# A decoder block on one core: the sixth head pair's transposes by VectorE and DMA instead of TensorE, and the out-projection's products ordered by feature halves

## The chip, the cores and the metric

The kernel runs on one core of a Trainium2 chip. Its engines work in parallel, each through its own instructions in order, and wait for each other by semaphores: TensorE (PE in the profile), VectorE (DVE), ScalarE (ACT), GpSimd (POOL) and SyncE (SP). SP and POOL also issue the transfers (DMAs) between the core's memory and HBM. The metric is the device time of one execution in microseconds (us), the median of several runs.

## The reference

One layer of a hybrid decoder: three groups of heads read one input projection, their outputs are concatenated and projected by `w_out`, and a feed-forward part follows. There are 512 tokens, width 1024, hidden width 4096, all in f32.

```python
h = rmsnorm(x, norm1_w)
proj = h @ w_in
aq, ak, av, bq, bk, bv, br, ba, cq, ck, cv = jnp.split(proj, ...)
y_a = dilated_attention(heads(aq, A_HEADS), heads(ak, A_HEADS), heads(av, A_HEADS), bias_a)   # 6 heads of 64
y_b = gla(heads(bq, B_HEADS), heads(bk, B_HEADS), heads(bv, B_HEADS), br, ba, w_a2, b_a, gla_norm_w)   # 4 heads
y_c = moba_attention(heads(cq, C_HEADS), heads(ck, C_HEADS), heads(cv, C_HEADS), bias_c)       # 6 heads of 64
mix = jnp.concatenate([y_a.reshape(Bsz, S, A_WIDTH), y_b, y_c.reshape(Bsz, S, C_WIDTH)], axis=-1)
x = x + mix @ w_out
h2 = rmsnorm(x, norm2_w)
x = x + jnp.square(jax.nn.relu(h2 @ w_ff1)) @ w_ff2
...
return rmsnorm(x, final_norm_w)
```

For 512 tokens both attentions come down to causal softmax attention with a bias table per head: the three dilated branches become one softmax whose bias holds the logarithm of how many branches see a distance, and the block-sparse attention sees every past block.

## The kernel before

**Order of the work.** The program is written as some thirty generators ("streams") that yield instructions, waits and fired events. At build time a planner (`Plan.run`) takes, with estimated costs, the instruction that can start first and issues it. So the order on each engine is fixed when the program is built, and on the chip each engine works through its list. All instructions are issued at one line (L141), which is why the profile's groups are told apart by the names of the tiles.

**Matrix products.** A product in f32 accuracy is made of three faster ones: each operand is cut into a high and a low part (ACT makes the high part: `wh`, `Ah`, `xh`; DVE the low part by a subtraction: `wl`, `Al`, `xl`), and hi x hi, lo x hi and hi x lo are summed in one PSUM bank. The out-projection and the second feed-forward matrix use a scheme with seven block products instead of eight (`products(c)`, c = 0 for the out-projection). Each product has a left operand that is a sum of blocks (`a_parts`, tiles `s`), a right operand that is a sum of weight blocks (`sums0`, tiles `t` and `b`; cut in `cut2`), and a bank X, W or Y in which it accumulates (`f2X`, `f2W`, `f2Y` in the profile). `add` puts a bank's result on the residual tiles `x3`, which the profile calls `x`. Each product runs over two halves of its inner dimension, `ip` = 0 and 1, 12 matmuls each.

**Attention.** The twelve heads of the two softmax attentions run as six pairs p, with e = 0, 1 in a pair. For each head `attention` makes the scores on PE (`sps`) and `softmax` the exponentials in tiles `P` (queries on partitions). For the product with the values, P has to be transposed. For the pairs in `XP` (0 to 4) this is `moved`: DVE transposes blocks of 32x32 (`tb`, `t2s`), SP writes them to HBM (`turn`), and POOL reads them back so that the blocks end up in transposed order (`thb`, `th`; twelve DMAs a pair, in `back`). Pair 5 takes the other way: PE transposes into a bank (`ptp`, 10 blocks for each of the two heads), and ACT copies it out (`turned`). The row sums go through HBM too (`zt`, `rzb`).

**Values.** `values` takes two pairs at a time: it waits for their transposes, takes banks "o" and "g" (`po` in the profile), runs the products, and `mix_out` (DVE) scales them by `rzb` into the mix tiles `h`. The features of the mix are in the order `KO`: feature block 6 is pair 4, block 7 is pair 5, and both are needed only in `ip` = 1 of the lower half.

**After it.** When a residual tile is final, `x2_out` makes the norm (`ssq`, `y`), PE transposes the normalized rows (`y_out`, `yps`), and the feed-forward part begins (`ff1_first`, bank `f`).

SP's list also holds all loads of weights (`woraw` for the out-projection, `wraw`, `w1raw`, `w2raw` for the feed-forward part) and of the residual, in `fetch`, `fetch0`, `fetch1` and `fetch2`. A DMA of SP also waits until the eighth one before it has landed, where that has not yet been waited for (SP has eight semaphores in turn).

Of the kernel before, what the change touches and what calls it, by code (L numbers as in the profile page):

```python
# [29 lines left out]
NC = 5  # L30
ZL, PL = 4.5, 3.2
XP = (0, 1, 2, 3, 4)
# [177 lines left out]
def hybrid_block_kernel(ctx: ExitStack, tc: tile.TileContext, x0_d, xT_d, x_d, w0_d, wv_d, wqk_d, w1_d, w2_d,  # L210
# [81 lines left out]
    def fetch():  # L292
        for key, src, n in pieces[1:]:
# [211 lines left out]

    def cut2(c):
        for o, (n, *_) in enumerate(products(c)):
# [6 lines left out]
            for ip in range(2):  # L514
                yield from parts(("2", c, n, ip), B[c][n][ip])
            fire(("cut2", c, n))
# [434 lines left out]
    def values():  # L951


        for ps_ in ((0, 1), (2, 3), (4, 5)):
# [35 lines left out]
            for _ in range(4 + (ps_[0] == 0) + 2 * (ps_[0] == 4)):  # L990
# [30 lines left out]
    def moved(p, e, P):  # L1021
# [19 lines left out]
        yield from back(th, d)  # L1041
        if both:
            yield from back(th2, d2)
# [179 lines left out]
    def x2_out(t, half):  # L1223
        both = t in ssq
        yield from square_sum(t, half)
        if both:
# [6 lines left out]
            scaled.append(t)  # L1233
            if len(scaled) == NT:
# [14 lines left out]
    def y_out(t, half, y0):  # L1249
        r = (("pt", "pt"), ("o", "g"))[t % 2][half]  # L1250
# [83 lines left out]
    def a_parts(c):  # L1334
# [4 lines left out]
        def split(n, src, sign=1):  # L1339
            for ip in range(2):  # L1340
# [38 lines left out]
        if not c:  # L1379
            yield ("wait", ("v", 1, 0))  # L1380
            yield ("prio", 1)
        yield from ready(0, 0)
# [3 lines left out]
        if not c:  # L1386
            yield ("wait", ("values", 2))
            yield ("prio", 0.5)
# [7 lines left out]
        if c:  # L1396
            yield from split(1, q10)
        yield from ready(1, 1)
        yield from urgent(3)
        if c in (0, NC - 1):  # L1400
            yield from split(6, q11)
        yield from urgent(4)
        s1 = yield from made("s1", q01, q11, OP.subtract if c else OP.add)
# [4 lines left out]
        yield from split(3, s1, -1 if c else 1)  # L1408
        give("big")
        yield from urgent(6)  # L1410
        if not c:
            yield from split(1, q10)
            s4 = yield from made("s4", q10, s2, OP.subtract)
        else:
            yield ("take", "big")
            s4 = big("s4", F32, (128, 2, 2, 256))
            s4 = [s4[:, ip] for ip in range(2)]
            for ip in range(2):
                yield DVE.scalar_tensor_tensor(s4[ip], q10[ip], -1.0, s2[ip], op0=OP.mult, op1=OP.subtract)
# [464 lines left out]
```

## Time and profile before

| | |
|---|---|
| median of 3 runs | 557.39 us (556.43 to 557.56) |
| the profiled execution | 556.4 us |
| its span, first to last instruction | 554.6 us |
| TensorE clock granted | 0.997 |
| PE busy | 546.1 us, 98% |
| DVE busy | 488.0 us, 88% |
| ACT busy | 351.2 us, 63% |
| POOL busy | 84.6 us, 15% |
| moved by DMA | 101.44 MB, mean 183 GB/s |

The profiled execution is 1.0 us below the median of the runs and 1.8 us longer than its span, so times from the trace are compared with 556.4, and a difference is then taken over to the median. A row of the trace gives an instruction's start and duration; matmuls overlap in the pipeline, so what one costs is read from start to start, or from a piece of the chain divided by its count (the profile counts a matmul of f32 operands twice, with x80 for 40).

### The profile page before, as it was taken

How to read it: one execution, taken by the hardware profiler on the slowest of the kernel's cores; microseconds unless marked ns; L12 is line 12 of the kernel's file. 1: busy time of each engine (PE TensorE's matmuls, PEld its weight loads, DVE VectorE, ACT ScalarE, POOL GpSimd, SP SyncE). 2: the span in 40 equal slices, each digit the busy share in tenths (PEclk: the TensorE clock that was granted, in tenths of full speed). 3: DMA queues.
4: the chain of work that ended last, by engine and by line, in shares of the span. 5: the costliest groups of instructions: out<-in, count | busy, mean ns of one | idle time of the engine just before them, and what ended most of it. 6: DMA issues, size and time to landing. Idle time of an engine off the chain costs nothing.

```text
span 554.6 us, 9438 instructions
## 1 busy us (share of the span) xinstructions
PE 546.1 (98%) x3530; PEld 484.8 (87%) x3530; DVE 488.0 (88%) x793; ACT 351.2 (63%) x588; POOL 84.6 (15%) x135
## 2 busy tenths in 40 slices
PE   9999999999999999999999999999999999999995
PEld 8987888888888888999988999988999888999884
DVE  6969998999987899899899858999589999588986
ACT  7746465668576546768855448864377753479654
POOL 7100000431524001100111100111000111202031
PEclk9999999999999999999999999999999999999998
DMA  8930304699998969803679714688815788937504
GB/s 314 392 136 2 110 6 132 215 281 253 273 285 275 316 201 376 171 1 115 152 157 281 212 72 153 152 221 234 228 38 190 160 223 230 212 79 209 106 1 152
DMA packets 33518, 101.44 MB, mean 183 GB/s; under 512 B 5026, under 2 KB 5712, under 8 KB 33472
## 3 DMA queue, kind: packets, MB, share of 16 engines
q1 hardware_dynamic: 24816, 73.76, 39.3%
q0 software_dynamic: 8368, 26.53, 24.5%
q8 instruction: 28, 0.46, 0.3%
q10 hardware_dynamic: 288, 0.53, 0.3%
q14 instruction: 18, 0.15, 0.1%
HBM read 92.11 MB, written 8.71 MB: 182 GB/s over the span
## 4 chain that ended last, share of the span: by engine, by line
PE 98%; DVE 1%; issue 0%; ACT 0%; DVEq 0%
PE f2X L141 19%; PE f1V L141 15%; PE qkps L141 12%; PE f2W L141 10%; PE vps L141 8%; PE f1W L141 7%; PE f2Y L141 5%; PE f L141 4%; PE f1X L141 4%; PE sps L141 3%; PE po L141 2%; PE av L141 2%; PE lp L141 1%; PE bk L141 1%; PE bq L141 1%; PE op L141 1%
## 5 line engine op out<-in xcount | busy, mean ns | idle before, releaser
L141 POOL DMA_DIRECT2D w2raw<-in_w x36 | 31.7, 907 | 301.9 <-DVE wl L141 199.1
L141 DVE TENSOR_TENSOR wl<-w2raw,wh 128x1024 fp32r<-128x1024 f32 x56 | 68.4, 1238 | 2.6 <-ACT wh L141 2.6
L141 ACT ACTIVATE wh<-w2raw 128x1024 fp32r<-128x1024 f32 x56 | 58.2, 1050 | 17.3 <-PE f2Y L141 12.5
L141 PE MATMUL f2X<-wh,Ah 128*128 128x512 f32 (+1 forms) x160 | 62.3, 390 | 0.0
L141 PE MATMUL f2X<-wh,Al 128*128 128x512 f32 (+1 forms) x160 | 61.9, 387 | 0.0
L141 PE MATMUL f2X<-wl,Ah 128*128 128x512 f32 (+1 forms) x160 | 61.9, 387 | 0.0
L141 ACT ACTIVATE wh<-w1raw 128x1024 fp32r<-128x1024 f32 x42 | 43.3, 1051 | 29.2 <-DVE w1raw L141 27.6
L141 DVE TENSOR_TENSOR wl<-w1raw,wh 128x1024 fp32r<-128x1024 f32 x42 | 50.8, 1222 | 12.3 <-ACT wh L141 12.3
L141 PE MATMUL f1V<-Uh,wl 128*128 128x256 f32 x168 | 47.6, 283 | 0.0
L141 PE MATMUL f1V<-Ul,wh 128*128 128x256 f32 x168 | 47.6, 283 | 0.0
L141 PE MATMUL f1V<-Uh,wh 128*128 128x256 f32 x168 | 47.6, 283 | 0.0
L141 ACT ACTIVATE h<-h 128x512 f32<-128x512 f32 x53 | 33.3, 629 | 17.8 <-DVE h L141 17.1
L141 PE MATMUL qkps<-xh,wh 128*128 128x512 f32 x96 | 38.1, 397 | 0.0
L141 PE MATMUL qkps<-xh,wl 128*128 128x512 f32 x96 | 37.5, 390 | 0.0
L141 PE MATMUL qkps<-xl,wh 128*128 128x512 f32 x96 | 37.5, 390 | 0.0
L141 ACT ACTIVATE P<-P,mn 128x512 f32<-128x512 f32 (+3 forms) x48 | 26.6, 556 | 15.6 <-DVE mn L141 15.4
L141 PEld LDWEIGHTS f2X<-wh,Ah 128*128 128x128 f32 x160 | 30.1, 188 | 6.9 <-issue 1.0
L141 DVE TENSOR_TENSOR wl<-wraw,wh 128x1024 fp32r<-128x1024 f32 (+1 forms) x32 | 34.5, 1087 | 1.5 <-ACT wh L141 1.4
L141 PEld LDWEIGHTS f2X<-wl,Ah 128*128 128x128 f32 x160 | 30.1, 188 | 6.1
L141 PEld LDWEIGHTS f2X<-wh,Al 128*128 128x128 f32 x160 | 30.1, 188 | 5.8
L141 ACT ACTIVATE Ah<-s 128x512 fp32r<-128x512 f32 x40 | 23.8, 623 | 15.8 <-DVE s L141 15.3
L141 PEld LDWEIGHTS f1V<-Uh,wh 128*128 128x128 f32 x168 | 32.3, 192 | 0.0
(297 smaller groups left out, 1675.7 us busy)
## 6 DMA issues: line engine op xcount, KB each, us to landing
w2raw<-in_w SPq DMA_DIRECT2D x42, 512.0 KB
w2raw<-in_w POOLq DMA_DIRECT2D x36, 512.0 KB, 7.0
w1raw<-in_w SPq DMA_DIRECT2D x28, 512.0 KB
wraw<-in_wqk SPq DMA_DIRECT2D x12, 512.0 KB
turn<-tb SPq DMA_DIRECT2D x10, 512.0 KB
thb<-turn POOLq DMA_DIRECT2D x40, 128.0 KB, 5.9
wraw<-in_wv SPq DMA_DIRECT2D x8, 512.0 KB
woraw<-in_w SPq DMA_DIRECT2D x8, 512.0 KB
```

The lines of the kernel that those rows point to most:

```text
L141: getattr(getattr(self.nc, op.eng), op.method)(*op.args, **op.kw)
```

## The change

- `XP` now holds pair 5 too: its blocks are transposed by DVE, written to HBM by SP, and read back, and there are no `ptp` transposes on PE and no copies from them on ACT. For this pair alone the twelve read-backs are issued by SP, not by POOL (`back`).
- `values` runs pairs 0 and 1, then 2 and 3 together, then pair 4 alone and pair 5 alone, the last two both in bank "o".
- The out-projection's products are cut into halves of the inner dimension where that matters (`segments`): 0 and 4 whole, then 6, 2 and 1 with `ip` = 0, then 6 and 2 with `ip` = 1, 3 whole, 1 with `ip` = 1, 5 whole. `cut2`, `ff2` and `a_parts` (a new `mixed_parts` for c = 0) follow that order, and the sums `s` are made half by half.
- Product 1's bank Y is now of kind "pt" (free, since `ptp` is gone) and no longer "s"; `y_out` swaps its two pairs of banks.
- The loads of the second half of the residual wait for pair 4's read-backs instead of for its values; the cut of one feed-forward weight tile waits until the fourth token tile is scaled; `half_dense` waits for its weight half only where it uses it.

```diff
-XP = (0, 1, 2, 3, 4)
+XP = (0, 1, 2, 3, 4, 5)
...
             if key[0] == "x3":
-                yield ("wait", ("values", 4 if key[2] else 2))
+                yield ("wait", ("thx", 4) if key[2] else ("values", 2))
...
             yield ("wait", ("raw", key))
+            if key == ("1", 0, 0, 1):
+                yield ("wait", ("scaled", 3))
...
+    def segments(c):
+
+        at = {n: o for o, (n, *_) in enumerate(products(c))}
+        return [(at[n], n, ips) for n, ips in (((0, (0, 1)), (4, (0, 1)), (6, (0,)), (2, (0,)), (1, (0,)), (6, (1,)), (2, (1,)), (3, (0, 1)), (1, (1,)), (5, (0, 1))) if not c else [(n, (0, 1)) for n in at])]
+
     def cut2(c):
-        for o, (n, *_) in enumerate(products(c)):
+        for o, n, ips in segments(c):
...
-        for ps_ in ((0, 1), (2, 3), (4, 5)):
+        for ps_ in ((0, 1), (2, 3), (4,), (5,)):
...
-    def back(dst, d):
+    def back(dst, d, p):
         n = d.shape[1]
         for k in range(4):
-            yield POOL.dma_start(dst[k * 32:k * 32 + 32].rearrange("p (a c) -> p a c", a=4),
+            yield (SP if p > 4 else POOL).dma_start(dst[k * 32:k * 32 + 32].rearrange("p (a c) -> p a c", a=4),
...
-        r = (("pt", "pt"), ("o", "g"))[t % 2][half]
+        r = (("o", "g"), ("pt", "pt"))[t % 2][half]
...
+            for _, n, ips in segments(0)[2:]:
+                for ip in ips:
+                    for i in range(2):
+                        yield ("wait", ("h", 0, 4 + 2 * ip + i))
+                    q10, q11 = (hs[0][1, ip][:, half] for half in range(2))
+                    if n == 2:
+                        yield DVE.tensor_tensor(s[1][ip], q01[ip], q11, op=OP.add)
+                        yield DVE.tensor_tensor(s[2][ip], s[1][ip], q00[ip], op=OP.subtract)
+                    if n == 5:
+                        yield DVE.tensor_tensor(s[4][ip], q10, s[2][ip], op=OP.subtract)
+                    yield from split(n, {6: (q11, q11), 1: (q10, q10)}.get(n) or s[{2: 2, 3: 1, 5: 4}[n]], ips=(ip,))
...
-        return (dict(X="mm", Y="s", W="s") if not c else dict(X="s", Y="mm", W="pt") if c < NC - 1 else dict(X="s", Y="pt", W="mm"))[b]
+        return (dict(X="mm", Y="pt", W="s") if not c else dict(X="s", Y="mm", W="pt") if c < NC - 1 else dict(X="s", Y="pt", W="mm"))[b]
...
         def half_dense(f, j):
             for k in range(KT):
                 kh = k // 4
+                yield ("wait", ("w", ("1", 0, f // 2, kh)))
...
-                for kh in range(2):
-                    yield ("wait", ("w", ("1", 0, f // 2, kh)))
...
-            for o, (n, b_, new, _) in enumerate(products(c)):
+            seens = {}
+            for o, n, ips in segments(c):
+                _, b_, new, _ = products(c)[o]
```

What that does to the orders is shown at three places. On PE, before, the values of pairs 4 and 5 stood together inside product 0 of the out-projection (the rows after `th_2009` are pair 5's, in wide products):

```order
L141 MATMUL f2X<-wl,Ah 128x512
L141 MATMUL po<-thb,v 64x128 x16
L141 MATMUL po<-th_2009,v 64x128 x4
L141 MATMUL po<-th,v 64x256 x2
L141 MATMUL po<-thb,v 64x384 x2
L141 MATMUL po<-thb,v 64x128 x2
L141 MATMUL po<-thb,v 64x512 x2
L141 MATMUL f2X<-wh,Ah 128x512
```

Now pair 4's values stand inside product 4, behind its ninth matmul, and pair 5's at its end, ahead of the first half of product 6. These are the rows around pair 5's (`th_2125` is pair 5's):

```order
L141 MATMUL f2W<-wh,Al 128x512
L141 MATMUL f2W<-wl,Ah 128x512
L141 MATMUL po<-thb,v 64x128 x16
L141 MATMUL po<-th_2125,v 64x128 x4
L141 MATMUL f2W<-wh,Ah 128x512
```

The values of the last two pairs moved from product 0 to product 4, fifteen matmuls of 512 columns apart from each other.

On SP, before, in the stretch behind the writes of pair 4 (`turn_2086` is its last; `x` are the residual's loads):

```order
L141 DMA turn_2086<-t2s 128x512
L141 DMA zt_2122<-rzt_99 8x32 x4
L141 DMA zt_2201<-rzt_101 8x32 x4
L141 DMA woraw<-in_w 128x1024 x2
L141 DMA rzb<-zt_2122 64x512 x2
L141 DMA rzb<-zt_2201 64x512 x2
L141 DMA x_2320<-in_x 128x512
```

And now (`turn_2164`, `turn_2195` and `turn_2204` are pair 5's):

```order
L141 DMA zt_2121<-rzt_99 8x32 x4
L141 DMA turn_2164<-tb 128x1024
L141 DMA woraw<-in_w 128x1024 x2
L141 DMA turn_2195<-tb 128x1024
L141 DMA turn_2204<-t2s 128x512
L141 DMA zt_2213<-rzt_101 8x32 x4
L141 DMA thb<-turn_2164 32x4x256 x4
L141 DMA rzb<-zt_2121 64x512 x2
L141 DMA thb<-turn_2195 32x4x256 x4
L141 DMA th_2125<-turn_2204 32x4x128 x4
L141 DMA x_2305<-in_x 128x512
```

The first load of the residual now stands behind three writes and twelve read-backs of pair 5; its row waits, by the eight semaphores, for the first read-back of `turn_2195`.

On DVE, before, from the copies of the values of pairs 2 and 3 to those of pairs 4 and 5 (`h<-po`):

```order
L141 TENSOR_TENSOR h<-po,rzb 128x2x256 x2
L141 TENSOR_TENSOR s_2319<-h 128x512 x2
L141 TENSOR_TENSOR wl<-b_2321,wh 128x1024
L141 TENSOR_TENSOR Al<-s_2319,Ah 128x512 x2
L141 TENSOR_TENSOR h<-po,rzb 128x2x256 x2
L141 TENSOR_TENSOR x_2320<-f2X,x_2320 128x512
```

And now, from the sums `s` behind the copies of pairs 2 and 3 to the copy of pair 4:

```order
L141 TENSOR_TENSOR s_2304<-h 128x512 x2
L141 TENSOR_TENSOR b_2314<-woraw,t_2170 128x1024
L141 TENSOR_TENSOR Al<-s_2304,Ah 128x512 x2
L141 TENSOR_TENSOR wl<-b_2308,wh 128x1024
L141 TENSOR_TENSOR Al<-h,Ah 128x512
L141 TENSOR_TENSOR s_2367<-h 128x512
L141 TENSOR_TENSOR wl<-t_2145,wh 128x1024
L141 TENSOR_TENSOR x_2305<-f2X,x_2305 128x512
L141 TENSOR_TENSOR x_2320<-f2X,x_2320 128x512
L141 TENSOR_TENSOR s_2368<-s_2367,h 128x512
L141 TENSOR_TENSOR Al<-s_2368,Ah 128x512
L141 TENSOR_TENSOR h<-po,rzb 128x2x256
```

The copy of pair 4 out of bank "o" now stands behind two adds of the residual, and PE's values of pair 5 wait for that copy.

More of the change, by code (lines that the diff above doesn't have):

```diff
@@ L513, in cut2 @@
             yield ("wait", ("B", c, n))
-            for ip in range(2):
+            for ip in ips:
                 yield from parts(("2", c, n, ip), B[c][n][ip])
+            if 1 not in ips:
+                continue
             fire(("cut2", c, n))
@@ L989, in values @@
             yield ops
-            for _ in range(4 + (ps_[0] == 0) + 2 * (ps_[0] == 4)):
+            for _ in range(2 * len(ps_) + (ps_[0] == 0) + 2 * (ps_[0] == 5)):
                 give("big")
@@ L1233, in x2_out @@
             scaled.append(t)
+            fire(("scaled", t))
             if len(scaled) == NT:
@@ L1337, in new, with split @@
             return slot(name, dt, (128, 2, 256))
-        def split(n, src, sign=1):
-            for ip in range(2):
+        def split(n, src, sign=1, ips=(0, 1)):
+            for ip in ips:
                 yield ("take", "part")
@@ L1377, in give_h, with mixed_parts @@
             give("big")
-        if not c:
+        def mixed_parts():
             yield ("wait", ("v", 1, 0))
             yield ("prio", 1)
+            yield from ready(0, 0)
+            yield from ready(0, 1)
+            q00, q01 = quad(0, 0), quad(0, 1)
+            yield from split(0, q00)
+            yield ("wait", ("values", 2))
+            yield ("prio", 0.5)
+            s3 = yield from made("s3", q00, q01, OP.subtract)
+            yield from split(4, s3)
+            give("big")
+            s = {}
+            for n in (1, 2, 4):
+                yield ("take", "big")
+                s[n] = big(f"s{n}", F32, (128, 2, 2, 256))
+                s[n] = [s[n][:, ip] for ip in range(2)]
+            for _, n, ips in segments(0)[2:]:
+                for ip in ips:
+                    for i in range(2):
[7 more added lines that the diff above has]
+                    yield from split(n, {6: (q11, q11), 1: (q10, q10)}.get(n) or s[{2: 2, 3: 1, 5: 4}[n]], ips=(ip,))
+                if n == 2 and 1 in ips:
+                    give_h()
+                if n == 3 and 1 in ips:
+                    give("big")
+            give("big")
+            give("big")
+            give_h()
+        if not c:
+            yield from mixed_parts()
+            return
         yield from ready(0, 0)
@@ L1395, in a_parts @@
         q10, q11 = quad(1, 0), quad(1, 1)
-        if c:
-            yield from split(1, q10)
+        yield from split(1, q10)
         yield from ready(1, 1)
         yield from urgent(3)
-        if c in (0, NC - 1):
+        if c == NC - 1:
             yield from split(6, q11)
         yield from urgent(4)
-        s1 = yield from made("s1", q01, q11, OP.subtract if c else OP.add)
+        s1 = yield from made("s1", q01, q11, OP.subtract)
         s2 = yield from made("s2", s1, q00, OP.subtract)
@@ L1407, in a_parts @@
         yield from urgent(5)
-        yield from split(3, s1, -1 if c else 1)
+        yield from split(3, s1, -1)
         give("big")
         yield from urgent(6)
[L1411 to L1419, printed above, removed]
+        yield ("take", "big")
+        s4 = big("s4", F32, (128, 2, 2, 256))
+        s4 = [s4[:, ip] for ip in range(2)]
+        for ip in range(2):
+            yield DVE.scalar_tensor_tensor(s4[ip], q10[ip], -1.0, s2[ip], op0=OP.mult, op1=OP.subtract)
         give("big")
@@ L1422, in a_parts @@
         give("big")
-        if c not in (0, NC - 1):
+        if c != NC - 1:
             yield from split(6, q11)
@@ L1709, in ff2 @@
                     elif m == 3:
-                        spawn(add(c, o, q, [bk[b_, q][h_] for h_ in js], [cut_[q][h_] for h_ in js]), -1 if end else 1 if c else 0)
+                        spawn(add(c, o, q, [bk[b_, q][h_] for h_ in js], [cut_[q][h_] for h_ in js]), -1 if end else 1 if c else 2 if n == 1 else 0)
     def main():
```

13 lines of the change are left out of this document (5 added, 8 removed).

## The prediction

> **What bounds the kernel now.** I read the page's busy shares and its chain first, then the waits of PE (TensorE), then busy time by stretches around the change, then the chain and the timelines of DVE (VectorE), SP and POOL in those stretches. The first fence has lines of the page (the one of ACT is used further down) and the one wait of PE outside the start.
>
> ```profile
> span 554.6 us, 9438 instructions
> PE 546.1 (98%) x3530; PEld 484.8 (87%) x3530; DVE 488.0 (88%) x793; ACT 351.2 (63%) x588; POOL 84.6 (15%) x135
> ...
> PE 98%; DVE 1%; issue 0%; ACT 0%; DVEq 0%
> ...
> L141 ACT ACTIVATE Ah<-s 128x512 fp32r<-128x512 f32 x40 | 23.8, 623 | 15.8 <-DVE s L141 15.3
> ...
> PE vps L141 <- ACT rg L141: 0.6, 1, 0.6
> ```
>
> PE is the bound, and nothing holds it up: 98% of the chain that ended last is its matmuls. So work taken off PE is worth its full time, as long as no new wait opens. Whether one opens is read from the stage that the change touches (busy time by stretches):
>
> ```profile
> core 0: us, PE busy (x) PEld busy (x) DVE busy (x) ACT busy (x) POOL busy (x), PEclk, DMA share, GB/s
> 160.00:175.00 15.00, 15.00 (x82) 12.83 (x81) 12.97 (x37) 11.63 (x34) 3.14 (x6) 1.00 0.88 284
> 175.00:185.00 10.00, 10.00 (x105) 8.62 (x105) 8.88 (x9) 4.40 (x5) 3.37 (x7) 1.00 1.01 245
> 185.00:195.00 10.00, 10.00 (x81) 7.43 (x80) 8.22 (x12) 7.09 (x9) 0.00 (x0) 1.00 1.04 370
> 195.00:210.00 15.00, 15.00 (x68) 12.43 (x67) 15.00 (x23) 6.90 (x13) 0.00 (x0) 1.00 0.62 201
> 210.00:225.00 15.00, 15.00 (x72) 12.50 (x71) 15.00 (x27) 9.97 (x23) 2.73 (x3) 1.00 1.01 355
> ```
>
> DVE has no gap at all from 195 to 225 us, and the DMA engines are full (share about 1.0) from 175 to 195. The change adds work to both and takes work from PE. The pieces of the chain there:
>
> ```profile
> 170.90 0.66 PE ptp L141 x6
> ...
> 179.52 0.68 PE f2X L141 x3
> 180.20 4.52 PE po L141 x80
> 184.72 1.58 PE f2X L141 x6
> 186.30 4.49 PE po L141 x56
> 190.78 3.67 PE f2X L141 x15
> 194.45 10.88 PE f2W L141 x48
> ...
> 221.65 0.87 PE yps L141 x8
> ```
>
> **PE's part.** Removed: the 20 transposes `ptp` of pair 5. Six take 0.66 us, 0.11 each, so 20 take 2.2 us. Changed: pair 5's values are now 20 narrow products instead of 8 wide ones. Pairs 2 and 3 need 4.52 us for both in the narrow form, 2.26 a pair; pairs 4 and 5 took 4.49 with one pair wide. So this costs nothing. Added: pairs 4 and 5 now interrupt the f2 products one at a time, three interruptions instead of two. A product of 512 columns takes 10.88/48 = 0.227 us; the six behind the first interruption took 1.58 instead of 1.36, the fifteen behind the second 3.67 instead of 3.40. So one more interruption costs 0.2 us. The products ordered by feature halves are the same 168 matmuls. PE's work: -2.2 + 0.2 = **-2.0 us**.
>
> **DVE's part.** Added: eight block transposes, four for each of the two heads. Their starts, and those of what follows, for pair 4 and in the last row of pair 5:
>
> ```profile
> 158.39 0.71 DVE L141 STREAM_TRANSPOSE tb<-P 128x512 f32<-128x512 f32 x1
> 159.02 0.65 DVE L141 TENSOR_TENSOR Al<-h,Ah 128x512 fp32r<-128x512 f32 x1
> ...
> 162.81 0.57 DVE L141 STREAM_TRANSPOSE tb<-P 128x384 f32<-128x384 f32 x1
> 163.31 0.40 DVE L141 STREAM_TRANSPOSE t2s<-P 128x256 f32<-128x256 f32 x1
> 163.63 0.27 DVE L141 STREAM_TRANSPOSE tb<-P 128x128 f32<-128x128 f32 x1
> 163.83 0.52 DVE L141 CUSTOM_DVE_ANT_0 P<-sps,nb 128x384 f32<-128x384 f32 x1
> ```
>
> Start to start they take 0.63, 0.50, 0.32 and 0.20, together 1.65 a head and 3.3 for the pair. Nothing is taken from DVE: the evictions of `ptp` were ACT's. What can cover 3.3 us is DVE's idle time ahead of its full stretch:
>
> ```profile
> 168.50 1.23 DVE L141 TENSOR_TENSOR t<-woraw 128x1024 f32<-128x1024 f32 x1 [0.29 <-DMA woraw<-in_w]
> ...
> 175.79 1.22 DVE L141 TENSOR_TENSOR wl<-woraw,wh 128x1024 fp32r<-128x1024 f32 x1 [2.22 <-ACT wh L141]
> ...
> 179.20 2.35 DVE L141 TENSOR_TENSOR t<-t,woraw 128x1024 f32<-128x1024 f32 x2
> 181.47 2.35 DVE L141 TENSOR_TENSOR b<-woraw,t 128x1024 f32<-128x1024 f32 x2
> ...
> 184.76 0.69 DVE L141 TENSOR_TENSOR h<-po,rzb 128x512 f32<-128x512 f32 x1 [0.34 <-PE po L141]
> 185.37 1.28 DVE L141 TENSOR_TENSOR s<-h 128x512 f32<-128x512 f32 x2
> ...
> 190.83 0.69 DVE L141 TENSOR_TENSOR h<-po,rzb 128x512 f32<-128x512 f32 x1 [1.24 <-PE po L141]
> 191.73 0.69 DVE L141 TENSOR_TENSOR x<-f2X,x 128x512 f32<-128x512 f32 x1 [0.21 <-PE f2X L141]
> ...
> 194.49 0.69 DVE L141 TENSOR_TENSOR x<-f2X,x 128x512 f32<-128x512 f32 x1 [0.33 <-PE f2X L141]
> ```
>
> The brackets add up to 4.63 us. So the transposes fit, but DVE gets ahead of its old schedule by at most 4.63 - 3.3 = 1.3 us, while PE wants to get ahead by 2.0. At the end of the full stretch PE takes the rows `y` of the norm at 221.65 us, and there is little slack there. Between those bounds, 1.3 and 2.0, I take 1.6 us, nearer to DVE's: DVE's row is the one without a gap. ACT loses evictions and is not short of time.
>
> **SP and the wait that it can bring.** Now SP issues three writes of pair 5 and twelve read-backs. All of them stand ahead of the eight loads of `x` (the residual), which stood at 177.47. Timelines of SP and POOL, and the landing times of pair 4's twelve read-backs (least, median, most):
>
> ```profile
> 145.65 0.33 SPq L141 DMA_DIRECT2D turn<-tb  x1
> ...
> 177.47 4.45 SPq L141 DMA_DIRECT2D x<-in_x  x4
> ```
> ```profile
> 152.22 0.55 POOL L141 DMA_DIRECT2D thb<-turn  x1 [2.70 <-DMA turn<-tb]
> ```
> ```profile
> DMA to landing us min/median/max: 2.9/7.6/8.4
> ```
>
> A write of 512 KB was issued at 145.65 and its read-back at 152.22, 6.6 us later. When do pair 5's last transposes end? In DVE's new order five of the eight stand ahead of the sum `t` that started at 168.50, and the last three behind it: 168.50 - 0.29 of idle + 2.28 + 1.13 (`t`) + 1.02 = 172.6. So read-backs could issue from 179.2; I take 181, since two 512 KB loads of the out-projection's weights now stand between the two heads' writes. SP's first `x` waits until the first read-back of the second head has landed (its row waits on that DMA's semaphore): 181 + 7.6 = 188.6. It lands 2.9 us later at the earliest, 191.5, or 8.4 later, 197. With every step at its short end it would be 179.2 + 2.9 + 2.9 = 185.0. I take 192, near the short end of the last step, because the traffic is then thinning out.
>
> Who waits for that: PE starts its f2X at 179.52 - 2.2 = 177.3. By the prices above: 0.68 + 4.52 + 21 x 0.227 = 187.3, nine f2W to 189.3, pair 4's values with the 0.2 to 191.8, fifteen f2W to 195.2. There pair 5's values need bank "o", which DVE must first empty of pair 4's, and in DVE's new order two adds of `x` stand ahead of that. DVE gets to the rows `s` at 185.37 - 2.85 of idle (0.29 + 2.22 + 0.34) - 1.13 (one sum `b` that moves behind) + 3.3 = 184.7. Then come three 1024-wide rows of 1.13 and six 512-wide of 0.61, to 191.7, and the first add of `x`. From there to an empty "o" stand two adds, `s`, ACT's split of 0.62, `Al` and the copy `h`, 3.8 us. With `x` landed at 192 that is 195.8, and PE waits **0.6 us**; with `x` in time, 0.3. The ends are 0 (DVE 0.3 faster than this count) and 197 + 3.8 - 195.2 = 5.6. This is the same late DVE that the 0.4 us above stands for, so I take the larger of the two, 0.6, and not their sum.
>
> The values themselves are not late by this: the last read-backs stand right ahead of `x` on SP, issue by 188.6 and land 2.9 us later, 191.5; PE needs them at 195.2. Taking the 12 read-backs on SP rather than on POOL costs POOL nothing; its later rows are loads that accumulate, far behind. The wait of `cut` for ("scaled", 3), the banks of `y_out` and of product 1, and the later wait in `half_dense` only move rows of DVE, ACT and PE; the matmul order from the first full feed-forward unit on is unchanged. I cost them at 0, covered by DVE's order.
>
> **Sum.** -2.2 (transposes) + 0.2 (third interruption) + 0.6 (DVE late at bank "o") = **-1.4 us**. The profiled execution took 556.4 us, so 555.0; the median of the three runs is 557.4, 1.0 above it, so **556.0 us** for the median.
>
> [...] The rows price a block's transpose at 0.11 us of PE and 3.3/20 = 0.165 us of DVE, plus two trips through HBM. [...]
>
> **Rivals.**
> - *The whole gain.* The loads land earlier and DVE's idle time covers the transposes in full: -2.0 to -2.2 us, 555.3. For it: PE never waited for DVE in this stage. Against it: 15.00 of 15.00 for DVE.
> - *Gain given back.* `x` lands between 192.4 and 194.5: PE waits 1 to 3.1 us, and the time is 556.4 to 558.5, within 0.2%. For it: share 1.0 of the DMA engines from 175 to 195, where 2.5 MB more must pass, at 245 to 370 GB/s another 7 to 10 us of traffic.
> - *Slower, by the queue.* SP's chain of write, read-back and `x` runs at its long end, with `x` at 197: PE waits 5.6 us, and the time is 557.4 - 2.0 + 5.6 = 561.0. It decides from 194.5 on (a wait of 3.1).
> - *Slower, by DVE.* The idle time is not usable: it lies behind waits for ACT and PE that stay. Then DVE ends its full stretch 3.3 us later than before, PE waits for it there whatever lead it had, and the time is 557.4 + 3.3 = 560.7; it decides where less than 2.2 of the 4.63 us can be used. [...] Against it: most of the 2.22 us was DVE waiting for an ACT that ran evictions of `ptp`, which are gone.
>
> **Chances.** What a measurement of this kernel can tell from no change is about 0.2%, 1.1 us. Forecast (gain 1.1 to 2.0): 0.37. Whole gain: 0.15. Given back: 0.35. Slower by the queue 0.07, by DVE 0.06. So faster 0.52, same 0.35, slower 0.13. The range 554.9 to 558.3 takes in the whole gain with 0.3 us of spread and the given-back case nearly to its end; it leaves out the queue's case and DVE's. The forecast's own range is 555.4 to 556.3.
>
> **What would show it.** Right: no `ptp` rows; PE's first f2X near 177.3; DVE without the 2.22 us gap; a small wait of PE at pair 5's `po`, ended by DVE `h`; the norm's first `yps` near 220. Wrong: a wait of DVE `x` for DMA x<-in_x of over 2 us (queue), PE waiting for the DMA of `thb` (read-backs late), or several waits of PE for DVE `Al`, `x` or `yl` between 195 and 230 (DVE the bound).

## The result, and the profile after

The changed kernel is slower: 561.09 us (560.19 to 561.58, four runs) against 557.34 of the kernel before (556.43 to 557.56, four runs), a ratio of 1.0069 with an interval of 1.0051 to 1.0086, +3.75 us. Medians and ratios leave out two executions that stand far off all others, one of e3 below (3091 us) and one of the kernel before in the comparison of e9 to e12 (1674 us). The profiled execution took 560.19 us with a span of 558.4, 3.8 more than before. The forecast was 556.0 with 554.9 to 558.3 as its range, so it is wrong in sign and the range does not hold the time.

From the page of the changed kernel: span, busy shares, what the DMAs moved, and the chain that ended last.

```profile
span 558.4 us, 9476 instructions
PE 546.4 (98%) x3534; PEld 484.1 (87%) x3534; DVE 490.9 (88%) x801; ACT 348.6 (62%) x582; POOL 84.7 (15%) x135
DMA packets 35678, 104.06 MB, mean 186 GB/s; under 512 B 5266, under 2 KB 7488, under 8 KB 35632
PE 88%; DVE 5%; ACT 2%; issue 1%; SPq 1%; DMA 1%; DVEq 0%; ACTq 0%
```

PE's busy time is about the same as before, but PE's share of the chain fell from 98% to 88%: DVE, ACT, SP and transfers now set the end in places where nothing but PE did. The DMAs moved 104.06 MB, 2.62 more than before; that is pair 5's trip through HBM. PE's waits (total, times, longest):

```profile
PE po L141 <- DVE h L141: 1.8, 1, 1.8
...
PE f2W L141 <- DVE x L141: 0.8, 1, 0.8
PE f L141 <- DVE yl L141: 0.7, 2, 0.5
PE vps L141 <- ACT rg L141: 0.6, 1, 0.6
PE f1V L141 <- ACT h L141: 0.5, 1, 0.5
```

Of these rows only the `vps` row was there before. The same stretches as in the prediction, and one more:

```profile
core 0: us, PE busy (x) PEld busy (x) DVE busy (x) ACT busy (x) POOL busy (x), PEclk, DMA share, GB/s
160.00:175.00 15.00, 15.00 (x72) 12.59 (x71) 14.74 (x46) 10.77 (x29) 2.73 (x6) 1.00 1.05 336
175.00:185.00 10.00, 10.00 (x105) 8.63 (x104) 10.00 (x12) 1.75 (x2) 3.82 (x7) 1.00 0.98 293
185.00:195.00 10.00, 10.00 (x75) 8.20 (x74) 7.94 (x11) 3.65 (x5) 0.00 (x0) 1.00 0.89 237
195.00:210.00 15.00, 12.41 (x83) 9.85 (x82) 12.23 (x16) 9.34 (x12) 0.00 (x0) 1.00 1.02 375
210.00:225.00 15.00, 15.00 (x67) 12.16 (x66) 14.81 (x26) 9.15 (x20) 2.28 (x3) 1.00 0.95 343
225.00:255.00 30.00, 29.13 (x222) 27.13 (x221) 26.04 (x41) 20.68 (x39) 1.33 (x2) 1.00 0.34 69
```

DVE filled its old gaps ahead of 185 us, as forecast (10.00 of 10.00 from 175 to 185). Then it stands idle: 2.1 us from 185 to 195 (1.8 before), and 2.8 from 195 to 210, where it had been full. The DMA engines, which had come down to a share of 0.62 from 195 to 210, are now full there (1.02). Who waits for whom is read from SP's, DVE's and PE's timelines:

```profile
178.11 6.16 SPq L141 DMA_DIRECT2D thb<-turn  x4
184.47 1.64 SPq L141 DMA_DIRECT2D rzb<-zt  x2
186.21 1.95 SPq L141 DMA_DIRECT2D thb<-turn  x4
188.20 1.85 SPq L141 DMA_DIRECT2D th<-turn  x4
190.15 1.81 SPq L141 DMA_DIRECT2D x<-in_x  x4
192.06 1.09 SPq L141 DMA_DIRECT2D rzb<-zt  x2
193.38 1.90 SPq L141 DMA_DIRECT2D x<-in_x  x4
```
```profile
193.09 0.69 DVE L141 TENSOR_TENSOR x<-f2X,x 128x512 f32<-128x512 f32 x1 [1.71 <-PE f2W L141]
194.14 0.69 DVE L141 TENSOR_TENSOR x<-f2X,x 128x512 f32<-128x512 f32 x1 [0.36 <-DMA x<-in_x]
...
196.18 0.69 DVE L141 TENSOR_TENSOR Al<-s,Ah 128x512 fp32r<-128x512 f32 x1 [0.76 <-ACT Ah L141]
196.79 0.68 DVE L141 TENSOR_TENSOR h<-po,rzb 128x512 f32<-128x512 f32 x1
...
200.08 0.69 DVE L141 TENSOR_TENSOR x<-f2W,x 128x512 f32<-128x512 f32 x1 [2.01 <-DMA x<-in_x]
```
```profile
197.53 2.03 PE L141 MATMUL po<-thb,v 128*64 128x128 f32 x31 [1.76 <-DVE h L141]
...
200.92 0.47 PE L141 MATMUL f2W<-wh,Ah 128*128 128x512 f32 x1 [0.81 <-DVE x L141]
```

SP's first load of `x` is issued at 190.15 instead of 177.47. It lands at 193.00, and DVE's add starts at 193.09 (the profile names PE f2W for that wait, but f2W had run for a microsecond by then). Behind it come the second load, ACT's split, `Al`, and at 196.79 the copy that empties bank "o", for which PE waits 1.8 us. Then DVE stands still again until 200.08, because the last four loads of `x`, issued from 193.38 on, are under way; the add at 200.08 needs the third of them, which landed at 199.99, and PE waits for that add too. The chain has both ends of it; of the rows left out between them, those from 186.38 to 194.42 are SP issuing its DMAs, most of them 0.43 to 0.48 us apart (e16 and e17 ask whether that is the cause):

```profile
177.55 0.68 PE f2X L141 x3
...
194.42 5.57 DMA x<-in_x
200.08 0.70 DVE x L141
200.78 0.14 issue
200.92 1.63 PE f2W L141 x6
```

Matched matmul by matmul (start times), PE's lead and loss against before read so:

| matmul | before us | after us | difference |
|---|---|---|---|
| first f2X | 179.36 | 177.39 | -1.97 |
| product 5 (f2X), sixth matmul from its end | 227.28 | 229.21 | +1.93 |
| first f (feed-forward) | 228.75 | 230.83 | +2.07 |
| last f ahead of f1V | 253.77 | 257.29 | +3.52 |
| f1V, start of its second run | 259.65 | 263.91 | +4.26 |

So the change wins 2.0 us up to 177, loses 3.9 by 229 (of it 1.9 and 1.0 at the two waits above, start to start; the other 1.0 was not taken apart), and another 2.3 in the norm and the first feed-forward unit. PE's last matmul is still 4.26 late; the span is only 3.8 longer, since the tail behind that matmul is 0.5 shorter, for a reason that was not looked for.

### The profile page after: what moved, and what is told of

The parts are those of the page before. It is cut to its first block, busy times and chain, and to the rows that moved or that the text cites. A ratio compares the mean times of both kernels' runs of the same rounds, so it can differ in the third digit from the quotient of the medians.

```text
span 558.4 us, 9476 instructions
## 1 busy us (share of the span) xinstructions
PE 546.4 (98%) x3534; PEld 484.1 (87%) x3534; DVE 490.9 (88%) x801; ACT 348.6 (62%) x582; POOL 84.7 (15%) x135
## 2 busy tenths in 40 slices
DMA packets 35678, 104.06 MB, mean 186 GB/s; under 512 B 5266, under 2 KB 7488, under 8 KB 35632
## 4 chain that ended last, share of the span: by engine, by line
PE 88%; DVE 5%; ACT 2%; issue 1%; SPq 1%; DMA 1%; DVEq 0%; ACTq 0%
PE f2X L141 17%; PE f1V L141 14%; PE qkps L141 12%; PE f2W L141 9%; PE vps L141 8%; PE f1W L141 7%; PE f2Y L141 4%; PE f1X L141 4%; PE sps L141 3%; PE av L141 2%; PE po L141 2%; SPq L141 1%; PE lp L141 1%; DVE y L141 1%; PE bk L141 1%
## 5 line engine op out<-in xcount | busy, mean ns | idle before, releaser
L141 PE MATMUL f2W<-wh,Ah 128*128 128x512 f32 x80 | 31.5, 393 | 0.8 <-DVE x L141 0.8
```

The source lines that it names most:

```text
L141: getattr(getattr(self.nc, op.eng), op.method)(*op.args, **op.kw)
```

## The experiments

All are built on the changed kernel ("after") unless said otherwise. A gain or loss in us is the median less the median of the kernel before in the same comparison. Theories on record: "x late" or "queue" (the residual's loads behind pair 5's transfers), "order" (the new order by itself), "DVE" (the transposes). Some profiles hold spells in which the granted clock is half, 3.4 us or 6.8 us long (in e9 the clock is 0.89 over the 15 us that hold one of 3.4 us: 1.65 us are short); by that one of 3.4 us takes PE back by up to 1.7 us, an estimate. They are named where they bear on a price, and the last section is on them.

**e1, the order without the transposes.**

```diff
-XP = (0, 1, 2, 3, 4, 5)
+XP = (0, 1, 2, 3, 4)
```

> The changed kernel without its transposes: pair 5 is turned by TensorE again (20 ptp), so SP has no writes and read-backs of pair 5 ahead of the loads of x; the orders by feature halves, the separate values of pairs 4 and 5 and the new banks stay. If the queue is the cause (x late behind the read-backs): x is on time, PE keeps only small waits, and the time is within 0.2% of before, 556.5 to 558.5 us (one interruption more, 0.2). If the 3.3 us of DVE transposes are the cause: the same. If the new order itself costs (DVE rows in an order that keeps PE waiting after 195 us): slower than before by over 1.1 us, 559 or more, with waits of PE for DVE in 195-260.

560.31 us, ratio 1.0058 (1.0044 to 1.0071), +3.3. The order alone, which I had costed at nothing, loses nearly as much as the whole change. Up to 1.7 us of that is the clock: the profile has a spell of 3.4 us at half clock from 233.8 (0.94 over the 30 us from 225 to 255), behind the waits below, and the two executions with a mean clock of 0.996 and 0.997 took 559.99 and 558.96, +3.0 and +1.9. Its waits do not lie at the residual but later, in the first feed-forward unit:

```profile
PE f L141 <- ACT wh L141: 0.9, 1, 0.9
PE f L141 <- DVE wl L141: 0.8, 1, 0.8
```

DVE lost its time before that, waiting for PE between the copies of pair 4 and pair 5, and had no gap from then on to 225:

```profile
194.01 0.69 DVE L141 TENSOR_TENSOR h<-po,rzb 128x512 f32<-128x512 f32 x1 [3.06 <-PE po L141]
```

**e2, the transposes without the order** (the kernel before, with pair 5 in `XP` and its read-backs on SP).

> The other half alone: pair 5 by VectorE and through HBM, read back from SP, with before's order of the out-projection and the values of pairs 4 and 5 together. Queue theory: the twelve read-backs still stand ahead of the loads of x on SP, x lands at 193 or later, and PE waits for DVE there as in the changed kernel: 559.5 to 562 us. DVE theory: the 3.3 us are there too, 560 to 561, but then with DVE full and no idle of DVE for x. Order theory: 555 to 556.5, the 2.2 us of PE gained.

561.66, ratio 1.0080 (1.0063 to 1.0096), +4.6. One wait, `PE f2W <- DVE x`, of 5.1 us: the `x` loads land up to 203.7, and product 4 needs its bank emptied on them. In the last of the wait a spell of 6.8 us at half clock begins (from 202.2; 0.77 over the 15 us from 195 to 210); PE works through 5.1 us of it, so up to 2.4 of the 4.6 us are the clock's. So each half of the change loses by itself, in another place, and the two losses do not add.

**e3, pair 5's read-backs on POOL's queue**, as for the other pairs, so that SP's list is free for `x`.

```diff
-            yield (SP if p > 4 else POOL).dma_start(...)
+            o = (SP if p > 4 else POOL).dma_start(...); o.emit = "gpsimd"; yield o   # the plan as for SP, issued by POOL
```

> The changed kernel with one edit: the twelve read-backs of pair 5 are issued by POOL, at the same place of the program; all other orders are the same row for row. SP then comes to x after its rzb loads, some 5 us earlier (about 185 instead of 190). Queue theory: the first x lands near 188 to 190 and the last near 195; DVE's idle for x (4.1 us in three places) goes, PE's waits of 1.9 and 1.0 us at 195-201 go or shrink below 0.5 each, and most of the 2.2 us of waits in 230-258 with them: 555.5 to 557.5 us. DVE theory: DVE is still 3.3 us behind, the waits move but stay: 559.5 to 561. DMA-traffic theory (the 4.0 MB more share the engines, whatever the queue): x lands at most 2 us earlier, 559 to 560.5.

562.45, ratio 1.0097 (1.0080 to 1.0114), +5.4, 1.7 us worse than the change; its profile has a spell of 3.4 us at half clock (0.83 over the 10 us from 195 to 205) that the change's has not (1.00). The first `x` lands at 189.7 instead of 193.0, but the last still at 201.5, and pair 5's blocks now come at 199.7, so PE waits for both (1.1 and 1.3 us). While the two queues run side by side, the DMA engines are full at a low rate:

```profile
185.00:195.00 10.00, 10.00 (x75) 8.20 (x74) 9.24 (x14) 4.56 (x7) 5.57 (x11) 1.00 1.05 238
```

**e4, DVE's transposes cut short** (one 32x32 block in each band instead of the row; POOL clears the tiles).

> The changed kernel in which the eight DVE transposes of pair 5 turn one 32 x 32 block a band only (about 0.07 us each in place of 0.2 to 0.63), with the tiles cleared by POOL, which is idle there; what pair 5 attends to is not computed. The writes, the read-backs, their queues and every order stay. DVE theory: 2.5 to 3 us come back, 557.5 to 558.5 us. Queue theory: the writes leave 1 to 2 us earlier at most, x lands at most 1 to 2 us earlier because SP waits for its earlier transfers to land, and 559 to 561 us remain.

560.84, ratio 1.0069 (1.0056 to 1.0081), +3.8 against +3.75. Taking away about 2.4 of DVE's 3.3 us (what is left takes some 0.9) brings nothing. (Its profile is a microsecond behind the change's before that can tell: the first short transpose starts at 168.21, where the change's full one starts at 167.24. And the waits at the residual are shorter, 1.3 instead of 2.6; e9 and e15 below ask without the traffic.) The rival "slower, by DVE" falls: transposing pair 5 on TensorE is the better choice here, 557.34 us against 561.09, but the 3.3 us of the VectorE transposes have no part in that.

**e5, after without pair 5's traffic** (no writes, no read-backs; POOL clears the tiles, so what pair 5 attends to is not computed), and **e6, e2 without it**.

```diff
-        yield SP.dma_start(d, t)
+        o = SP.dma_start(d, t); o.emit = None if p == 5 else o.emit; yield o    # planned, not issued
```

> The changed kernel without pair 5's way through HBM: its DVE transposes stay, its three writes and twelve read-backs are left out, and POOL clears the tiles that they would fill (what pair 5 attends to is not computed). Orders of TensorE, VectorE and ScalarE are the same row for row. Traffic theory (2.5 MB more through full DMA engines make x late by 5 to 6 us, on whatever queue): x lands by 195, DVE's 4 us of idle for x go, PE's waits at 195-201 (3.1 us) go, and, as DVE then reaches the norm earlier, most of the waits in 230-258 (2.2 us): 555.5 to 557 us. Order theory (the order alone cost 3.3 us in the run without transposes): only the 3.1 us at 195-201 go, 557.5 to 559. DVE theory: DVE is 3.3 us late all the same, 559.5 or more.

> The same leaving out of pair 5's writes and read-backs, but with before's order of the out-projection and the values of pairs 4 and 5 together; the DVE transposes stay. Traffic theory: x is on time, the wait of 5.1 us at 198 and the slower clock behind it (2.2 us) go, and the 2.2 us of TensorE's transposes are the gain: 554.8 to 556 us. If the 3.3 us on DVE are not covered: up to 3.3 us of waits between 195 and 230, 556.5 to 558.5.

e5: 558.22, ratio 1.0021 (1.0012 to 1.0029), +1.0; e6: 557.11, ratio 1.0004 (0.9994 to 1.0014), -0.1. The traffic is worth 2.7 us in the new order, where neither profile has a spell of half clock, and 4.7 in the old, of which up to 2.4 is e2's spell. But without it the change still does not win its 2.0. In e5 both waits at the residual are gone, and DVE has short gaps in its full stretch, 2.3 us between 192 and 216:

```profile
193.68 0.69 DVE L141 TENSOR_TENSOR Al<-s,Ah 128x512 fp32r<-128x512 f32 x1 [0.76 <-ACT Ah L141]
...
198.26 0.69 DVE L141 TENSOR_TENSOR h<-po,rzb 128x512 f32<-128x512 f32 x1 [0.36 <-PE po L141]
...
208.04 0.69 DVE L141 TENSOR_TENSOR x<-f2W,x 128x512 f32<-128x512 f32 x1 [0.34 <-PE f2W L141]
209.40 0.69 DVE L141 TENSOR_TENSOR x<-f2W,x 128x512 f32<-128x512 f32 x1 [0.67 <-PE f2W L141]
```

Against before, PE stands at -1.9 us at the first f2X, -1.1 in product 5 and +1.6 at f1V, at the matmuls of the table above: it is given back in the norm, where PE waits for DVE's `y`, `yl` and ACT's `h`. In e6 DVE has no gap from 174 to 202, and PE runs into it once: `PE f2W <- DVE x` of 2.0 us, behind three splits `wl` of DVE.

**e7, e1 with the values of pairs 4 and 5 together again.**

```diff
-        for ps_ in ((0, 1), (2, 3), (4,), (5,)):
+        for ps_ in ((0, 1), (2, 3), (4, 5)):
```

> The new order without the transposes, as in the run of the order alone, but with the values of pairs 4 and 5 together again; the halves, the wait of the cut for the fourth scaled tile and the banks stay. If the separate values are what costs in the order (DVE stood 3.06 us for pair 5's po there and was behind from then on): 557 to 558.3 us, DVE idle under 1.5 us around 190-194. If the rest of the order costs (the late split of w1, behind the norm): 559.5 to 561 again, with PE's waits for ACT wh and DVE wl near 230.

558.44, ratio 1.0024 (1.0013 to 1.0035), +1.25. Of e1's +3.3, 2.0 go when the two pairs are together again. By e1's two executions of higher clock taking them apart costs 0.5 to 1.6 of it; the rest is the half clock, of which e7's profile shows no spell there (1.00 from 225 to 255).

**e8, all loads of `x` ahead of pair 5's last writes on SP.**

```diff
-                yield ("wait", ("thx", 4) if key[2] else ("values", 2))
+                yield ("wait", ("sent", 4))
```

> The changed kernel with the same bytes in another order: all eight loads of x stand on SP ahead of the last writes of pair 5, at about 173 us, and its read-backs behind them. If only x's place in the queue counts: x lands by 187, no waits for x, 556 to 557.5 us. Traffic theory (the bytes that must be through by 200 us are too many, whichever goes last waits): x is early, but the read-backs of pair 5 land 4 to 6 us later, near 196 to 199, and PE waits for them at pair 5's po: 558.5 to 561 us.

566.60, ratio 1.0167 (1.0153 to 1.0182), +9.4. `x` is there by 191.2, pair 5's blocks only from 198.7 to 205.2, and an `Al` of DVE waits 5.5 us for the write of `t2s`, which now stands behind the loads. It says that the wait moves to whatever comes last, but with the `Al`, and with spells of 6.8 and 3.4 us at half clock behind the waits (0.81 over the 15 us from 195 to 210, 0.89 from 210 to 225), it is no clean measure of the price.

**e9, e6 with the short transposes of e4.**

> Before's order of the out-projection; pair 5's writes and read-backs are left out as in the run without traffic, and its eight DVE transposes turn one block a band only (what pair 5 attends to is not computed). If the DVE transposes ate the gain in the run without traffic in before's order (557.1, with a wait of TensorE of 2.2 us at 197 for DVE's x): that wait goes and the 2.2 us of ptp are left, 554.8 to 555.6 us. If something else made that wait (the loads of x, the order of the adds): 556.5 to 557.5.

558.72, ratio 1.0016 (1.0004 to 1.0029). The wait of e6 stands as it was:

```profile
PE f2W L141 <- DVE x L141: 2.0, 1, 2.0
```

DVE begins its full stretch at 174.7 in e6 and 174.8 in e9, with or without the transposes, because without them it waits there for ACT's `wh` (1.13 us). So the work taken out ahead of that point was free: the cover that the prediction claimed is real. That e9 is 1.6 us above e6 is not DVE's doing but the clock's; see the end.

**e10, after with the values together again** (the edit of e7).

> The changed kernel with the values of pairs 4 and 5 in one interruption again; the transposes, the traffic, the halves and the wait of the cut for the fourth scaled tile stay. If the separate values are what costs in the stage of the norm (the order alone went from 560.3 to 558.4 with joint values): 558.5 to 560 us, and the waits of 2.3 us between 229 and 264 go. If they only moved the waits: 560.5 to 562, since the wait for x then comes earlier for both pairs.

560.88, ratio 1.0054 (1.0037 to 1.0072), +3.6. The loss in the norm is gone: PE is 4.8 us late in product 5 and 5.1 at f1V. In its place stand a longer wait at the residual, since PE gets there sooner, and a spell of 3.4 us at half clock behind it (from 203.4; 0.89 over the 15 us from 195 to 210):

```profile
PE f2W L141 <- DVE x L141: 4.2, 2, 3.8
```

**e11, after without the wait of `cut` for ("scaled", 3).**

> The changed kernel without the one wait that it adds in cut (the split of the second piece of w1 for the fourth scaled tile); the order up to the norm stays, behind it DVE's and ACT's rows stand in another order. If that wait makes the 2.3 us of waits between 229 and 264: 558.5 to 559.5 us. If those waits come from DVE being late, or from other rows: 560.5 to 561.5.

559.96, ratio 1.0051 (1.0039 to 1.0063), +2.7. PE's lag at f1V in the profile is the change's, 4.3 us, but by another way: this execution waited 3.1 us at bank "o" and had a spell of 3.4 us at half clock in the same stretch (0.89 over the 15 us from 195 to 210). The interval overlaps that of the change; whether this wait costs up to a microsecond stays open.

**e12, the kernel before with only one head of pair 5 by DVE and HBM** (the other's keys are taken in reversed order within a block, the same work).

> Before with one head of pair 5 turned by VectorE and through HBM (1.65 us of DVE, 0.75 MB written and read), the other by TensorE; before's order. TensorE is rid of 10 transposes, 1.1 us. If traffic and DVE each have half the room that the whole pair needs (DVE could take 3.1 of its 4.6 us idle; x was 4.5 us early at its first add): the gain stays, 555.8 to 556.6 us. If each byte makes the last loads of x late: x's last loads land 4 us later, TensorE waits 1 to 2 us for DVE's x near 198, and 557 to 558.5.

558.93, ratio 1.0036 (1.0021 to 1.0051), +1.6: 1.57 MB more than before instead of 2.62, a wait `PE f2W <- DVE x` of 1.3 us, and the last `x` at 199.5. The wait grows faster than the bytes (e2 has 5.1 us); that the first of the delay is eaten by slack would explain it, and is not shown.

**e13, e6 with three of DVE's splits `wl` of feed-forward weights cut to 64 columns**: those ahead of the `x` adds.

> As the run without traffic in before's order (557.1 us; TensorE waits 2.2 us at 197 for DVE's x), with three more of DVE's rows made short: the splits wl of the out-projection that stand at 193.1, 195.5 and 197.3 there take 64 of 1024 columns (about 0.1 in place of 1.2 us each; POOL clears the rest, so these low parts are not computed). If DVE, full from 175 us on, is what eats the 2.2 us that TensorE is rid of: DVE reaches x some 2 us earlier, the wait at 197 shrinks below 0.5 and 554.6 to 555.6 us come out, the whole gain. If the wait has another cause (x's landing at 192 to 194, the banks): it stays, 556.8 to 557.5.

555.54, ratio 0.9974 (0.9965 to 0.9983), -1.6, and the wait of e6 is gone. About 3.2 us of DVE work taken out of this stretch bring 1.5: there DVE bounds the kernel beside PE.

**e14, the kernel before with only the values taken apart.**

> Before with one edit: the values of pairs 4 and 5 are two interruptions instead of one (pair 5 still by TensorE's transposes, the old order of the products). If the separate values are what costs in the new order: 558.5 to 560 us, with waits of TensorE behind 195. If they cost only in the new order's spacing (fifteen f2W between them, where the planner puts three or four f2X here): within 0.2% of before, 556.3 to 558.3.

557.14, ratio 1.0006 (0.9997 to 1.0015), 0.0. There the two pairs stand within product 0 with nine f2X between them, and the price is nil; it is 3.0 us where fifteen f2W of product 4 stand between them (e5 against e15 below).

**e15, e10 without pair 5's traffic.**

> The new order with joint values and the DVE transposes, without pair 5's writes and read-backs (what pair 5 attends to is not computed). It completes the table: with the old order this was 557.1, with the new order and separate values 558.2. If the separate values make the 2.7 us of waits in the norm (229 to 264): 555.5 to 557 us. If they only carry DVE's lateness to another place: 557.5 to 558.5.

555.11, ratio 0.9971 (0.9959 to 0.9983), **-2.0**. This is the whole gain that the count of PE's matmuls had promised. No wait at the residual is left, and DVE is full:

```profile
185.00:195.00 10.00, 10.00 (x105) 8.66 (x104) 10.00 (x15) 6.23 (x9) 0.00 (x0) 1.00 1.03 349
195.00:210.00 15.00, 15.00 (x67) 12.40 (x67) 14.93 (x20) 9.84 (x13) 0.00 (x0) 1.00 0.71 252
```

**e16 and e17, the loads of `x` on POOL's queue**, in e10 (e16) and in the change itself (e17): two queues instead of one. The rival that this asks after is SP's issuing: from 185 to 195 the DMA engines were busy for only 0.89 of the time in the change and 0.71 in e10.

```diff
-                yield SP.dma_start(x3[key[1:]], src)
+                o = SP.dma_start(x3[key[1:]], src); o.emit = "gpsimd"; yield o
```

> The new order with joint values (560.9 us; 555.1 without pair 5's traffic), with one edit: the eight loads of x are issued by POOL, which is idle from 183 us on, instead of by SP behind its twelve read-backs. All orders else are the same. If SP's issuing, one transfer each 0.48 us, is what makes x late (the DMA engines were busy 0.71 of 185-195 there): x lands by 192 and 196, the waits of 4.2 us for x go, 555.5 to 557.5 us, faster than the changed kernel and perhaps than before. If the bytes are: x is earlier, but the read-backs land 3 us or more later and PE waits for them at the values instead: 559 to 562 us.

> The changed kernel itself with the loads of x issued by POOL. SP-issue theory: x lands by 192 and 196, the 3.1 us of waits at 195-201 go, and 558 to 559 us are left, as without traffic (558.2; the separate values remain). Bytes theory: pair 5's read-backs land later, near 195, which its values at 195 can just take; the second four loads of x land near 198 to 200 all the same: 559.5 to 561 us.

e16: 563.21, ratio 1.0111 (1.0098 to 1.0124); e17: 562.21, ratio 1.0091 (1.0076 to 1.0107). Both are worse than with one queue; each profile's mean clock is below that of the one-queue kernel's (0.991 against 0.993, 0.994 against 0.997), so the size of the loss is not clean. The engines are full from 185 to 195 now (1.04 and 1.03), `x` is there by 199.0 and 198.6, and pair 5's blocks come by 200.7 and 201.1. The waits are for those (in e17 the profile names `rzb`, whose loads landed only at 201.4 and 202.1, after the wait's end at 200.3; the last of pair 5's `thb` had landed at 200.2):

```profile
PE po L141 <- DMA thb<-turn: 5.9, 1, 5.9
```
```profile
PE po L141 <- DMA rzb<-zt: 2.2, 1, 2.2
```

**The four corners**, all with pair 5 by DVE and in the new order, as gain or loss in us:

| | without the traffic | with it | price of the traffic |
|---|---|---|---|
| values together | -2.0 (e15) | +3.6 (e10) | 5.6 |
| values apart | +1.0 (e5) | +3.75 (the change) | 2.7 |
| price of taking apart | 3.0 | 0.2 | |

By the medians the two prices overlap. Waiting would explain it: both are DVE, or PE behind it, standing still in the same thirty microseconds, and whoever waits already does not wait again. But part of it, perhaps all, is the clock: e10's two executions at a mean clock of 0.997 and 0.999 took 559.45 and 557.9, +2.1 and +0.6, and by these two alone the 5.6 would be 2.6 to 4.1, and the 0.2 would be 1.6 to 3.2. The clean corners are e15, e5 and the change, whose profiles have no such spell: 3.0 for taking apart, 2.7 for the traffic.

**Is it the place in a queue, or the bytes?** When the last transfer of each kind lands, from the trace's DMA records:

| kernel | `x` on | read-backs on | last `x` us | last read-back us |
|---|---|---|---|---|
| before | SP | none | 194.5 | |
| after | SP, last | SP | 200.7 | 192.4 |
| e10 | SP, last | SP | 202.0 | 194.3 |
| e3 | SP | POOL | 201.5 | 199.7 |
| e17 | POOL | SP | 198.6 | 201.1 |
| e16 | POOL | SP | 199.0 | 200.7 |
| e5, no traffic | SP | none | 193.2 | |

In these rows whichever goes last, by one queue or by two, is through at 200.7 to 202.0; e2's last `x` came later, at 203.7, and e8's last blocks at 205.2. The 2.62 MB more, at the 370 GB/s of the busiest row of before, are 7.1 us, and 194.5 + 7.1 = 201.6; at the 237 GB/s of the change from 185 to 195 they are 11.1, and 205.6. The kernels named lie between these ends or up to 0.9 ahead of them, and e12 with 1.57 MB (198.7 to 201.1) has 199.5. So it is the bytes in the main; which queue, and in what place, moves the end by up to 4.5 us, and why the rate falls while the blocks move was not taken further.

## Why the prediction was wrong, step by step

- **PE's part, -2.0: right.** PE's first f2X starts at 177.39 (177.3 forecast), no `ptp` rows are left, and e15 shows the full 2.0 at the end.
- **DVE's part, 3.3 us under cover: right.** 10.00 of 10.00 from 175 to 185 us; e4 and e9 gain nothing where the transposes are cut, and e15 has the full gain with the transposes whole.
- **DVE late at bank "o", 0.6: right mechanism, wrong size.** It is 1.8 us. Of the difference 0.7 came from the way from the first `x` to an empty bank, 3.8 by my count and 4.5 by the trace (193.00 to the copy's end), with 0.36 of it a wait for the second load; 1.0 from `x` landing at 193.0 instead of 192; and PE itself was there 0.4 later than forecast (195.6, not 195.2).
- **The failed step at the residual: only the first loads were followed.** The text asks when the first `x` lands. The last four, which product 4's bank needs, were not priced; they land up to 200.7, and the wait for them costs another 1.0. The rival "slower, by the queue" has this mechanism and nearly this time (561.0), but its deciding point, the first `x` after 194.5, was at the wrong load: it decided by the last ones with the first at 193.0. That its 561.0 lies so near the measured 561.09 is luck: it has one wait of 5.6, where the change has 1.9 and 1.0 at the residual and 2.3 in the norm. Its sign did come (DVE `x` waits 2.01 us for a load of `x`). And "given back" had noted the 7 to 10 us of traffic; carried to the last `x`, 194.5 + 7 = 201.5, the row would have shown the wait.
- **The failed step on the order: costed at 0.2 for three interruptions, and at 0 for the rest.** The 0.2 is PE's price of an interruption. DVE's was left out: taken apart, the two copies out of bank "o" and what follows each of them make DVE wait for PE, and DVE had been full ("no gap at all", as the prediction itself read). That is 3.0 us without the traffic (e5 against e15), 2.0 with `ptp` (e1 against e7, of which 0.5 to 1.6 without the half clock), and it falls due in the norm, thirty microseconds behind the cause. In the change itself undoing it alone brings 0.2 by the medians (e10), within the measurement: the 2.0 us of the norm go, and a longer wait for `x` and the half clock behind it take their place.
- **The chances.** 0.13 for slower was too little. A chain that is 98% PE told that PE was the bound; it did not tell that DVE had no slack from 195 to 225, though the stretches did (15.00 of 15.00, twice).

What stays open: the 2.3 us between 229 and 264 in the change. With the values together they shrink to 0.3 (e10 and e15), so they come with the values apart; which gap of DVE's or ACT's carries how much was not taken further.

No version tried wins with the real transfers; those that do leave them out. What would win, by e15, is pair 5 transposed off PE without the 2.62 MB in this stretch and with its values beside pair 4's; no run has that with pair 5's real values.

## What to carry to other kernels

Where an engine is the chain at 98%, look in each stage for the engine that is second: one with 15.00 of 15.00 was a bound too here, and where a new order makes it wait, that can come out, perhaps much later, as a wait of the first (here 2.3 us of DVE's gaps, and 2.7 us of PE's in the norm, thirty microseconds on, in e5). A trip through HBM can be priced by its bytes at the rates that the stretch shows (here 237 to 370 GB/s), added to when the last transfer already there lands; here neither another place in the queue nor a second queue brought the end ahead of that sum by more than a microsecond, they changed who waits. Follow all the loads behind the inserted ones to their users, not the first.

## What the runs showed of the hardware

Behind waits of PE the granted clock was half for a while in some profiles and stayed full in others, and the mean clock differs between executions of one program. The first rows are PE's in e2 after its wait, then a stretch of e9 and the same one of e6:

```profile
203.95 0.76 PE L141 MATMUL f2W<-wh,Ah 128*128 128x512 f32 x1 [5.12 <-DVE x L141]
204.52 0.63 PE L141 MATMUL f2W<-wh,Al 128*128 128x512 f32 x1
204.94 0.63 PE L141 MATMUL f2W<-wl,Ah 128*128 128x512 f32 x1
205.37 0.63 PE L141 MATMUL f2W<-wh,Ah 128*128 128x512 f32 x1
...
209.15 0.39 PE L141 MATMUL f2W<-wh,Ah 128*128 128x512 f32 x1
209.37 0.39 PE L141 MATMUL f2W<-wh,Al 128*128 128x512 f32 x1
```
```profile
195.00:210.00 15.00, 12.99 (x60) 10.22 (x57) 12.71 (x19) 6.30 (x9) 0.00 (x0) 0.89 0.68 241
```
```profile
195.00:210.00 15.00, 12.98 (x57) 10.44 (x57) 14.22 (x21) 7.28 (x12) 0.00 (x0) 1.00 0.63 234
```

Products of 512 columns stand 0.427 us apart instead of 0.227 until 209. In e9 this happens after a wait of only 2.0 us (from 201.5 to 204.9; the 0.89 of the stretch is 1.65 us short of full in these 3.4 us, so about half), in e6 after the same wait not at all (1.00). It is not the kernel: of e6's twelve executions nine had a mean clock of 0.995 to 0.997 and took 556.4 to 557.7 us, three had 0.993 and took 558.5 to 559.1; of e9's eight, two had 0.997 (556.7 and 556.9) and six 0.993 or 0.994 (558.5 to 559.1). So a wait of 2 us cost either itself or 2 us more. e10's six go the same way, from 557.9 at a clock of 0.999 to 561.7 at 0.991, and its price of 5.6 above holds about 2 of this kind.

The other profiles show no length of wait that decides. There is a spell of 3.4 us behind, or beginning in, waits of 0.9 and 0.8 us (e1, from 233.8), 3.8 (e10, from 203.4) and 5.9 (e16, from 199.2), one in the same stretch as waits of 1.1 and 1.3 (e3, 0.83 over the 10 us from 195 to 205) and of 3.1 (e11, 0.89 over the 15 us from 195 to 210), and one of 6.8 beginning in waits of 5.1 (e2, from 202.2) and 5.4 (e8, from 194.0). There is none behind 1.3 (e12), 2.0 (e6) and 2.2 (e17), each with 1.00 in the stretch, nor behind the change's 1.8 and 0.8: its profile shows 1.00 in every stretch, its runs 0.995 to 0.997. The profiles of e2, e16 and e17 have mean clocks of 0.988, 0.991 and 0.994; their stretches from 160 to 255 explain 0.006, 0.003 and nothing of what is short, and before, without a spell in any of these stretches, has 0.997, so in each another 0.003 or so, about 1.7 us, is short outside them. A wait of 2.0 us brought the half clock in six executions of e9's eight, by their mean clocks, and why in these is not shown.
